# A linear recurrence with its GpSimd steps moved to ScalarE and VectorE, and four memory-query units moved

## The chip, the cores and the metric

The kernel runs on one core of one Trainium2 chip. The metric is the device time of one execution in microseconds. The inputs are fp32; the large products are formed from a high and a low part of each operand (three matmuls for one product).

## The reference

The network is two transformer-like blocks behind each other over 1024 positions of width 1024. The first has two layers: one whose mixer is windowed attention, and one whose mixer is a gated linear recurrence (LRU). Beside each mixer stands a memory attention over 256 memory rows. The second block has a stick-breaking attention and a sliding window. Only the recurrent layer matters here:

```
p = h @ w_in;  xb, gate, mq = split(p)
xc = centred_depthwise_conv(xb, conv_w, conv_b)          # 4 taps
for each direction d (forward, backward):
    r = sigmoid(xc @ wa[d] + ba[d]);  i = sigmoid(xc @ wx[d] + bx[d])   # block-diagonal, 8 blocks of 128
    log_a = -8 * r * softplus(-lam[d]);  a = exp(log_a)
    u = sqrt(-expm1(2 * log_a)) * (i * xc)
    h[t] = a[t] * h[t-1] + u[t]                           # over 1024 positions
y = (h_forward + h_backward) * gelu(gate)
mo = softmax(mq @ mk / sqrt(128)) @ mv                    # 4 heads
x = x + concat(y, mo) @ w_out;   then an MLP
```

`-expm1(2 log_a)` is computed in the kernel as `(a*a + 1) * tanh(8 r softplus)`.

## The kernel before, in words

All tiles have the 128 partitions as channels and up to 1024 positions along the free axis. The recurrent layer runs over 8 channel blocks `c` of 128. For each block there are four helpers:

- `lru_p` loads two weight pieces (512 KB each), splits each into a high and a low part (VectorE does both for these), and runs 4 x 24 = 96 matmuls of 128x512 into the tile `psx`; ScalarE copies the results to `xb` (convolution input) and `gl` (gate).
- `lru_c` is the convolution (VectorE, lines 902 and 905), and the split of its result into `xch` and `xcl`.
- `lru_g` is the gates: 24 matmuls into `psg` (8 results, each in one of the three PSUM banks with the tag `S`), and 8 sigmoids on ScalarE (line 923).
- `lru_e` is the recurrence: for both directions `exp` (line 932) and `tanh` (933) on ScalarE, the square of `a` (935) and the product `i*xc` (937) on GpSimd, `(sq+1)*r` (936) on VectorE; then `gelu` (939) and two `sqrt` (941) on ScalarE, the product `i*r` (945) and the two scans (947, 949) on VectorE, the sum of both directions (952) on GpSimd, and the product with the gate (953) and the split into `yh` and `yl` on VectorE and ScalarE, which go to DRAM.

In the sources `lru_p` of block c+1 stands before `lru_g` of block c, and `lru_c` of block c+1 before `lru_e` of block c. The sigmoids, exponentials, tanh, gelu and sqrt are tied into one order on ScalarE by `chain`, since ScalarE loads another function table at each change of function set. The rest of the order on each engine comes from the framework's scheduler, which orders instructions by their place in the sources and by simulated times.

The buffers matter. The tags `r` and `i` have three tiles each, and a block needs two of each: the second direction of block c+1 can write its gates only when the first direction's tiles of block c are free, `r` after line 952, `i` (which becomes `y`) after the split into `yl`. The tag `sq` has one tile.

The memory attention has 8 units (4 heads x 2 halves of the positions) from `mem_units`: `part_p` is the query (24 matmuls into `psq`, split into `mqh` and `mql`), `part_s` the scores (12 matmuls into `ms`, in two banks of the tag `S`; line 381 is the exponential), `part_b` transposes and the product with the values. In the sources units 0 to 3 have their queries in the last block, before its `lru_e`, and the scores of unit 0 too; the other four queries stand in the loop behind the recurrence.

After that `down_groups` multiplies with `w_out` (tile `psd`) in three groups of four 128-channel chunks: channels 0 to 511 of the recurrence, channels 512 to 1023, memory. Its first two groups load their input into the SBUF tiles that held the layer's input `hh`, `hl`, so they can be loaded only when the last query matmul has read these.

Of the kernel before, what the change touches and what calls it, by code (L numbers as in the profile page):

```python
# [47 lines left out]
def net_kernel(ctx: ExitStack, tc: tile.TileContext, xT, memT, vecs, pos, sinks, invf, mask0, maskc, alibi,  # L48
# [286 lines left out]

    def mem_units(l, hh, hl, pieces, tp, psp, order, qtag=("mqh", "mql")):
        sc = 1.0 / math.sqrt(128.0)
# [27 lines left out]
        def part_s(h, th, qh, ql):  # L365
# [5 lines left out]
            for u in range(2):  # L371
# [7 lines left out]
                for j in range(2):  # L379
                    t = 2 * u + j  # L380
                    act.activation(p[:, t, :], s2[:, j, :], AF.Exp, bias=mx[:, t:t + 1], scale=sc,
                                   accum_out=sm[:, t:t + 1])
            dve.reciprocal(sm, sm)
# [440 lines left out]
    sp8 = cp.tile([P, 16], F32, tag="sp8", name="sp8")  # L824
    nsp8 = cp.tile([P, 16], F32, tag="nsp8", name="nsp8")

    def softplus(tk):
# [17 lines left out]
        dve.tensor_scalar(out=sp8, in0=sp8, scalar1=8.0, scalar2=None, op0=ALU.mult)  # L845
        dve.tensor_scalar(out=nsp8, in0=sp8, scalar1=-1.0, scalar2=None, op0=ALU.mult)

    cond = cp.tile([P, 8], F32, tag="cond", name="cond")
# [8 lines left out]
    for l in range(2):  # L857
        if l == 1:

            with ExitStack() as ph:  # L860
# [66 lines left out]
                def lru_e(c, xc, gl, ri):  # L927
                    av = []
                    for d in range(2):
                        r, ii = ri[d]  # L930
                        a = T.tile([P, S], F32, "a", nm("a"))
                        chain(act.activation(a, r, AF.Exp, scale=nsp8[:, 8 * d + c:8 * d + c + 1]))
                        chain(act.activation(r, r, AF.Tanh, scale=sp8[:, 8 * d + c:8 * d + c + 1]))
                        sq = T.tile([P, S], F32, "sq", nm("sq"))
                        pool.tensor_tensor(out=sq, in0=a, in1=a, op=ALU.mult)
                        dve.scalar_tensor_tensor(out=r, in0=sq, scalar=1.0, in1=r, op0=ALU.add, op1=ALU.mult)
                        pool.tensor_tensor(out=ii, in0=ii, in1=xc, op=ALU.mult)
                        av.append(a)
# [12 lines left out]
                    y = ri[0][1]  # L951
                    pool.tensor_tensor(out=y, in0=ri[0][0], in1=ri[1][0], op=ALU.add)
                    dve.tensor_tensor(out=y, in0=y, in1=gl, op=ALU.mult)
# [6 lines left out]

                M = Tags({"mqh": mq, "mql": mq}, {"st": 12, "pt": 4, "mqh": 4, "mql": 4})
                mus = mem_units(1, hh, hl, w_mq[4:8], M, psp, [(i // 2, i % 2) for i in range(8)])
                pq = []
                pn = lru_p((0, 1))
                cn = lru_c(0, pn[0][0])
                for c in range(KC):
                    gl, cc = pn.pop(0)[1], cn
                    if 0 < c < KC - 1:
                        pn += lru_p((c + 1,))
                    ri = lru_g(c, cc[1], cc[2])  # L970
                    if c + 1 < KC:
                        cn = lru_c(c + 1, pn[0][0])
                    else:
                        pq = [mus[i][2]() for i in range(4)]
                        mem_units.load_w(2)
                        pre.close()
                        mk = side_pool(ph, "amk", "right")
                        M.pool.update({tag: mk for tag in ("mkh", "mkl", "mv", "mP", "st")})
                        nxt = mus[0][3](pq[0])
                    lru_e(c, cc[0], gl, ri)  # L980
                lru.close()
                xe = side_pool(down, "x1e", "left")
# [3 lines left out]
                for i in range(8):  # L986
                    cur = nxt
                    if i < 8 - 4:
                        pq.append(mus[4 + i][2]())
                    if i < 7:  # L990
# [470 lines left out]
```

## Time and profile before

| | |
|---|---|
| median of 3 runs | 3113.42 us (3112.48 to 3114.47) |
| the profiled execution's own time | 3114.57 us |
| its span, first to last instruction | 3112.6 us |
| TensorE matmuls busy | 2994.6 us, 96% |
| VectorE busy | 1803.7 us, 58% |
| ScalarE busy | 1300.7 us, 42% |
| GpSimd busy | 391.9 us, 13% |
| mean granted TensorE clock | 0.981 |

The recurrent mixer, from its first matmul to the first one of its output projection, runs from 1261 to 1590 us of the span. TensorE's busy time counts pipelined matmuls that overlap, so the share of busy time overstates how full it is: how many matmuls start in a stretch tells more.

### The profile page before, as it was taken

To read this page: it belongs to the slowest core of one execution; us is meant where nothing else is said; L and a number is where in the kernel's file an instruction comes from. 1 tells how busy PE (TensorE), PEld (TensorE's weight loads), DVE (VectorE), ACT (ScalarE), POOL (GpSimd) and SP (SyncE) were. 2 spreads that over 40 slices of the span, in tenths; PEclk is the share of its full clock that TensorE was granted. 3 is DMA by queue.
4 is the path that set the end of the run, shared out by engine and by line. 5 is a ranking of instruction groups with operands and counts; after the bars stand their busy time and mean duration, and the time that the engine had idled before them with its cause. 6 is when DMAs were issued, how large, how long until landed. Compare 5 with 4: busy or idle time off the path is not lost. (4 is left out here: it accounts for less than half of the span.)

```text
span 3112.6 us, 38989 instructions
## 1 busy us (share of the span) xinstructions
PE 2994.6 (96%) x14688; PEld 2430.1 (78%) x14688; DVE 1803.7 (58%) x3071; ACT 1300.7 (42%) x2390; POOL 391.9 (13%) x426
## 2 busy tenths in 40 slices
PE   8999999799999999999889889999999899999998
PEld 7888778678888888777667768888888677777777
DVE  8666754774456542788764674445243745555555
ACT  6566541544542221366751444451121433334442
POOL 3222100300000000243310300000001201111102
PEclk9999999999999999999999989999999899999999
DMA  7111354343365432221263333354231210111142
GB/s 265 36 55 55 101 194 150 125 149 102 108 215 194 143 115 71 68 68 65 78 254 139 119 129 109 109 181 151 68 123 54 81 55 35 35 35 48 62 176 75
DMA packets 136348, 341.61 MB, mean 110 GB/s; under 512 B 14944, under 2 KB 29664, under 8 KB 136160
## 3 DMA queue, kind: packets, MB, share of 16 engines
q1 hardware_dynamic: 131840, 331.93, 31.1%
q10 hardware_dynamic: 4320, 7.20, 0.7%
q8 instruction: 115, 1.88, 0.2%
q14 instruction: 73, 0.60, 0.1%
HBM read 245.22 MB, written 93.85 MB: 109 GB/s over the span
## 5 line engine op out<-in xcount | busy, mean ns | idle before, releaser
L122 PE MATMUL psd<-uh,wh 128*128 128x512 f32 (+1 forms) x1568 | 606.2, 387 | 2.5 <-DVE mql L105 1.7
L126 PE MATMUL psd<-uh,wl 128*128 128x512 f32 (+1 forms) x1568 | 606.5, 387 | 0.0
L125 PE MATMUL psd<-ul,wh 128*128 128x512 f32 (+1 forms) x1568 | 606.3, 387 | 0.0
L104 ACT CAST wh<-wr 128x1024 fp32r<-128x1024 f32 (+2 forms) x236 | 234.7, 998 | 730.6 <-PE psd L125 506.3
L105 DVE TENSOR_TENSOR wl<-wr,wh 128x1024 fp32r<-128x1024 f32 (+2 forms) x260 | 314.4, 1212 | 218.1 <-ACT wh L104 216.9
L316 DVE TENSOR_TENSOR x<-x,psd 128x512 f32<-128x512 f32 x288 | 196.1, 685 | 377.7 <-PE psd L126 372.6
L122 PEld LDWEIGHTS psd<-uh,wh 128*128 128x128 f32 x1568 | 294.6, 188 | 63.8 <-issue 2.3
L126 PEld LDWEIGHTS psd<-uh,wl 128*128 128x128 f32 x1568 | 294.6, 188 | 60.7 <-issue 2.6
L125 PEld LDWEIGHTS psd<-ul,wh 128*128 128x128 f32 x1568 | 294.6, 188 | 59.7 <-issue 1.7
L122 PE MATMUL psu<-oph,wh 128*128 128x512 f32 x512 | 200.4, 394 | 41.1 <-ACT wh L104 41.1
L154 POOL TENSOR_TENSOR acc<-acc,sq 128x512 f32<-128x512 f32 (+1 forms) x70 | 95.8, 1369 | 1009.5 <-ACT sq L150 998.3
L125 PE MATMUL psu<-opl,wh 128*128 128x512 f32 x512 | 199.8, 391 | 0.0
L126 PE MATMUL psu<-oph,wl 128*128 128x512 f32 x512 | 198.6, 390 | 0.0
L125 PE MATMUL pj<-hl,wh 128*128 128x512 f32 x416 | 166.1, 404 | 8.0 <-DVE hl L105 8.0
L122 PE MATMUL pj<-hh,wh 128*128 128x512 f32 x416 | 168.4, 409 | 2.5 <-DVE qkl L105 1.3
L126 PE MATMUL pj<-hh,wl 128*128 128x512 f32 x416 | 167.0, 406 | 0.0
L122 PEld LDWEIGHTS psu<-oph,wh 128*128 128x128 f32 x512 | 96.6, 189 | 62.4 <-ACT wh L104 42.0
L125 PEld LDWEIGHTS psu<-opl,wh 128*128 128x128 f32 x512 | 96.7, 189 | 20.3 <-issue 0.5
L126 PEld LDWEIGHTS psu<-oph,wl 128*128 128x128 f32 x512 | 96.6, 189 | 20.3
L1201 DVE TENSOR_TENSOR_SCAN om<-om 128x128 f32<-128x128 f32 (+7 forms) x64 | 86.0, 1352 | 38.5 <-ACT om L1197 38.3
L122 PE MATMUL psx<-hh,wh 128*128 128x512 f32 x256 | 99.0, 397 | 4.8 <-ACT gl L897 4.8
L122 PE MATMUL psu<-oph,vh 128*128 128x512 f32 x256 | 100.7, 393 | 0.0
(337 smaller groups left out, 6027.9 us busy)
## 6 DMA issues: line engine op xcount, KB each, us to landing
wr<-in_w_up SPq DMA_DIRECT2D x64, 512.0 KB, 3.8
ud<-cc SPq DMA_DIRECT2D x128, 256.0 KB, 2.2
ur<-ud SPq DMA_DIRECT2D x64, 512.0 KB, 3.4
wr<-in_w_down SPq DMA_DIRECT2D x64, 512.0 KB, 4.1
wr<-in_w_out SPq DMA_DIRECT2D x32, 512.0 KB, 3.6
wr<-in_w_in SPq DMA_DIRECT2D x26, 512.0 KB, 3.5
wra<-in_w_ada SPq DMA_DIRECT2D x24, 512.0 KB, 4.3
uh<-mixh SPq DMA_DIRECT2D x20, 512.0 KB, 7.6
```

Source lines behind the costliest of these rows:

```text
L104: act.copy(hi, src)
L105: lo_eng.tensor_tensor(out=lo, in0=src, in1=hi.bitcast(F32), op=ALU.subtract)
L122: ins = pe.matmul(out, lh, rh, start=start and i == 0, stop=False, skip_group_check=skip)
L125: pe.matmul(out, lh, rl, start=False, stop=False, skip_group_check=skip)
L126: ins = pe.matmul(out, ll, rh, start=False, stop=stop and i == n - 1, skip_group_check=skip)
L154: pool.tensor_tensor(out=self.acc[:, :n], in0=self.acc[:, :n], in1=sq[:, :n], op=ALU.add)
L316: dve.tensor_tensor(out=xs, in0=xs, in1=ps, op=ALU.add)
L1201: dve.tensor_tensor_scan(out=om[:, :nk][:, ::-1], data0=om[:, :nk][:, ::-1], data1=om[:, :nk][:, ::-1], initial=1.0, op0=ALU.mult, op1=ALU ...
```

## The change

The square of `a` becomes a second exponential of the same `r` on ScalarE (with twice the factor, kept in a new small tile `nsp16`). The products `i*xc` and the sum of both directions become VectorE instructions. GpSimd keeps only the memsets in this stage. `chain` now also holds the exponentials of this layer's memory attention, in the order of the sources. The queries of units 0 and 1 move to block 3, those of units 2 to 5 to the last block, 6 and 7 stay in the loop behind; the tags `mqh` and `mql` get 6 tiles in place of 4; the scores of unit 0 move behind the last `lru_e`, and the early load of a third query weight (`load_w(2)`) goes.

```diff
-    def mem_units(l, hh, hl, pieces, tp, psp, order, qtag=("mqh", "mql")):
+    def mem_units(l, hh, hl, pieces, tp, psp, order, qtag=("mqh", "mql"), chain=lambda ins: None):
...
-                    act.activation(p[:, t, :], s2[:, j, :], AF.Exp, bias=mx[:, t:t + 1], scale=sc,
-                                   accum_out=sm[:, t:t + 1])
+                    chain(act.activation(p[:, t, :], s2[:, j, :], AF.Exp, bias=mx[:, t:t + 1], scale=sc,
+                                         accum_out=sm[:, t:t + 1]))
...
+        dve.tensor_scalar(out=nsp16, in0=sp8, scalar1=-2.0, scalar2=None, op0=ALU.mult)
...
                     for d in range(2):
                         r, ii = ri[d]
                         a = T.tile([P, S], F32, "a", nm("a"))
+                        sq = T.tile([P, S], F32, "sq", nm("sq"))
                         chain(act.activation(a, r, AF.Exp, scale=nsp8[:, 8 * d + c:8 * d + c + 1]))
+                        chain(act.activation(sq, r, AF.Exp, scale=nsp16[:, 8 * d + c:8 * d + c + 1]))
                         chain(act.activation(r, r, AF.Tanh, scale=sp8[:, 8 * d + c:8 * d + c + 1]))
-                        sq = T.tile([P, S], F32, "sq", nm("sq"))
-                        pool.tensor_tensor(out=sq, in0=a, in1=a, op=ALU.mult)
+                        dve.tensor_tensor(out=ii, in0=ii, in1=xc, op=ALU.mult)
                         dve.scalar_tensor_tensor(out=r, in0=sq, scalar=1.0, in1=r, op0=ALU.add, op1=ALU.mult)
-                        pool.tensor_tensor(out=ii, in0=ii, in1=xc, op=ALU.mult)
...
-                    pool.tensor_tensor(out=y, in0=ri[0][0], in1=ri[1][0], op=ALU.add)
+                    dve.tensor_tensor(out=y, in0=ri[0][0], in1=ri[1][0], op=ALU.add)
...
-                M = Tags({"mqh": mq, "mql": mq}, {"st": 12, "pt": 4, "mqh": 4, "mql": 4})
-                mus = mem_units(1, hh, hl, w_mq[4:8], M, psp, [(i // 2, i % 2) for i in range(8)])
+                M = Tags({"mqh": mq, "mql": mq}, {"st": 12, "pt": 4, "mqh": 6, "mql": 6})
+                mus = mem_units(1, hh, hl, w_mq[4:8], M, psp, [(i // 2, i % 2) for i in range(8)], chain=chain)
...
                     else:
-                        pq = [mus[i][2]() for i in range(4)]
-                        mem_units.load_w(2)
                         pre.close()
                         mk = side_pool(ph, "amk", "right")
                         M.pool.update({tag: mk for tag in ("mkh", "mkl", "mv", "mP", "st")})
-                        nxt = mus[0][3](pq[0])
+                    pq += [mus[i][2]() for i in {3: (0, 1), 7: (2, 3, 4, 5)}.get(c, ())]
                     lru_e(c, cc[0], gl, ri)
+                nxt = mus[0][3](pq[0])
...
-                    if i < 8 - 4:
-                        pq.append(mus[4 + i][2]())
+                    if i < 2:
+                        pq.append(mus[6 + i][2]())
```

## Rows read from the trace of the kernel before

**Rows 1.** The page: span, busy time of each engine.
```profile
span 3112.6 us, 38989 instructions
PE 2994.6 (96%) x14688; PEld 2430.1 (78%) x14688; DVE 1803.7 (58%) x3071; ACT 1300.7 (42%) x2390; POOL 391.9 (13%) x426
```

**Rows 2.** Busy time by stretch of the span (from:to, length, then PE, PEld, DVE, ACT, POOL busy us with instruction counts, granted TensorE clock, DMA share, GB/s): one full stretch, the ramp of the recurrent mixer, three stretches of two blocks each, its end, and what comes behind.
```profile
1300.00:1340.00 40.00, 40.00 (x178) 33.14 (x177) 26.55 (x25) 19.24 (x24) 8.64 (x7) 1.00 0.21 66
...
1261.00:1354.00 93.00, 88.92 (x388) 72.24 (x387) 67.27 (x74) 40.01 (x54) 20.99 (x19) 0.98 0.16 51
1354.00:1419.00 65.00, 56.24 (x231) 44.93 (x230) 57.27 (x40) 43.24 (x52) 25.46 (x14) 0.94 0.20 69
1419.00:1484.00 65.00, 58.30 (x236) 47.01 (x235) 56.46 (x41) 42.82 (x51) 25.51 (x12) 0.92 0.21 73
1484.00:1548.00 64.00, 55.94 (x228) 44.10 (x227) 49.67 (x35) 48.74 (x59) 23.96 (x11) 0.95 0.23 79
1548.00:1590.00 42.00, 33.91 (x163) 28.14 (x163) 30.39 (x44) 29.85 (x50) 14.10 (x6) 0.88 0.42 140
1590.00:1740.00 150.00, 147.92 (x678) 118.08 (x677) 69.77 (x129) 38.33 (x83) 9.44 (x7) 1.00 0.51 189
```

**Rows 3.** Groups of TensorE instructions between 1261 and 1590 us (busy us, mean ns, idle time just before them and who ended it).
```profile
L122 PE MATMUL psx<-hh,wh 128*128 128x512 f32 x256 | 99.0, 397 | 4.8 <-ACT gl L897 4.8
L122 PE MATMUL psg<-xch,wh 128*128 128x512 f32 x64 | 27.6, 442 | 18.7 <-ACT r L923 18.7
L122 PE MATMUL psq<-hh,wh 128*128 128x512 f32 x64 | 26.6, 416 | 2.7 <-DVE mql L105 2.7
L122 PE MATMUL ms<-mkh,mqh 128*128 128x256 f32 x18 | 5.5, 321 | 8.1 <-ACT mp L381 7.7 <-ACT a L932 0.4
```

**Rows 4.** GpSimd in order of time: the sum of both directions, line 952, which comes once in each block (first, third, seventh and eighth of 8; start us, length us).
```profile
1354.10 2.39 POOL L952 TENSOR_TENSOR i<-r,r 128x1024 f32<-128x1024 f32 x1 [8.87 <-DVE r L949]
...
1419.20 2.37 POOL L952 TENSOR_TENSOR i<-r,r 128x1024 f32<-128x1024 f32 x1 [7.54 <-DVE r L949]
...
1547.54 3.23 POOL L952 TENSOR_TENSOR i<-r,r 128x1024 f32<-128x1024 f32 x1 [9.74 <-DVE r L949]
...
1584.45 2.39 POOL L952 TENSOR_TENSOR i<-r,r 128x1024 f32<-128x1024 f32 x1 [16.23 <-DVE r L949]
```

**Rows 5.** One period, 1419 to 1452 us, on GpSimd, VectorE (DVE) and ScalarE (ACT): rows of the three engines' lists, put in order of time (start us, length us).
```profile
1421.53 2.41 POOL L937 TENSOR_TENSOR i<-i,xc 128x1024 f32<-128x1024 f32 x1
1421.60 3.42 DVE L953 TENSOR_TENSOR i<-i,gl 128x1024 f32<-128x1024 f32 x1 [2.55 <-POOL i L952]
1427.05 1.28 ACT L923 ACTIVATE i<-psg,vec 128x512 f32<-128x512 f32 x2
1429.29 1.28 ACT L932 ACT_TABLE_LOAD   x1
1430.58 1.16 ACT L932 ACTIVATE a<-r,nsp 128x1024 f32<-128x1024 f32 x1
1431.88 2.75 POOL L935 TENSOR_TENSOR sq<-a 128x1024 f32<-128x1024 f32 x1 [0.68 <-ACT a L932]
1437.68 1.22 DVE L936 SCALAR_TENSOR_TENSOR r<-sq,r 128x1024 f32<-128x1024 f32 x1
1439.04 2.80 POOL L935 TENSOR_TENSOR sq<-a 128x1024 f32<-128x1024 f32 x1 [4.41 <-DVE r L936]
1444.04 1.21 DVE L936 SCALAR_TENSOR_TENSOR r<-sq,r 128x1024 f32<-128x1024 f32 x1
1445.29 1.06 ACT L941 ACTIVATE r<-r 128x1024 f32<-128x1024 f32 x1 [5.07 <-DVE r L936]
1449.43 2.28 DVE L949 TENSOR_TENSOR_SCAN r<-a,i 128x1024 f32<-128x1024 f32 x1
```

**Rows 6.** Groups of instructions between 1300 and 1600 us on VectorE and ScalarE, in the same columns as rows 3.
```profile
L945 DVE TENSOR_TENSOR i<-i,r 128x1024 f32<-128x1024 f32 x16 | 25.5, 1593 | 3.1 <-ACT r L941 3.1
L953 DVE TENSOR_TENSOR i<-i,gl 128x1024 f32<-128x1024 f32 x8 | 25.0, 3131 | 17.0 <-POOL i L952 17.0
L105 DVE TENSOR_TENSOR xcl<-xc,xch 128x1024 fp32r<-128x1024 f32 x8 | 18.2, 2273 | 2.8 <-ACT xch L104 2.8
L105 DVE TENSOR_TENSOR wl<-wr,wh 128x1024 fp32r<-128x1024 f32 x20 | 32.1, 1607 | 4.4 <-ACT wh L104 3.9
L923 ACT ACTIVATE r<-psg,vec 128x512 f32<-128x512 f32 x32 | 20.5, 685 | 31.2 <-POOL i L952 28.3 <-PE psg L126 2.9
L932 ACT ACTIVATE a<-r,nsp 128x1024 f32<-128x1024 f32 x16 | 18.3, 1146 | 0.1
```

**Rows 7.** The last block on ScalarE in order of time: three of the four table loads that lie between its exponentials of the memory attention (line 381) and its square roots (941).
```profile
1567.02 1.28 ACT L381 ACT_TABLE_LOAD   x1
...
1571.72 1.28 ACT L381 ACT_TABLE_LOAD   x1
...
1576.36 1.28 ACT L941 ACT_TABLE_LOAD   x1
```

**Rows 8.** TensorE in order of time: the last matmul of the last query, the last score matmul ahead of the output projection, and the projection's first matmul.
```profile
1586.81 0.39 PE L126 MATMUL psq<-hh,wl 128*128 128x512 f32 x1
...
1589.59 0.28 PE L126 MATMUL ms<-mkh,mql 128*128 128x256 f32 x1
1589.70 0.39 PE L122 MATMUL psd<-uh,wh 128*128 128x512 f32 x1
```

More of the change, by code (lines that the diff above doesn't have):

```diff
@@ L825, in net_kernel @@
     nsp8 = cp.tile([P, 16], F32, tag="nsp8", name="nsp8")
+    nsp16 = cp.tile([P, 16], F32, tag="nsp16", name="nsp16")
     def softplus(tk):
```

## The prediction

> **What bounds the kernel now.** I read the page first: TensorE's matmuls are busy for 96% of the span [rows 1], which looks as if nothing but TensorE counted. The table by stretch corrects that for the recurrent mixer. A stretch in which TensorE never rests starts 178 matmuls in 40 us, 0.225 us each [rows 2]. The three stretches from 1354 to 1548 us start 231 + 236 + 228 = 695 matmuls, worth 156 us, in 194 us: 38 us are lost, at a granted clock of 0.92 to 0.95. From 1548 to 1590 us 163 matmuls, at most 37 us of work, take 42 us at 0.88. Behind 1590 us TensorE is full again at 1.00. So this stage is not bound by TensorE, and a shorter recurrence can show in the time; all matmuls before 1590 us are 256x3 + 64x3 + 64x3 of 0.225 us and 54 scores of half the size [rows 3], some 265 us of 329. The gain can't be more than the 64 us that are left.
>
> What TensorE waits for there are the gate sigmoids (18.7 us) and, at the end, the exponentials of the scores (7.7 us) [rows 3]. ScalarE's sigmoids in their turn wait for GpSimd's sum of both directions, 28.3 us [rows 6], because the gates of the next block need the `r` tile which that sum is the last to read. So the stage is a ring: sum, gates, exponentials, squares, roots, scans, sum. Its period comes from the start times of the sum [rows 4]: (1547.54 - 1354.10) / 6 = 32.24 us, and 36.91 us for the last block. TensorE's own work in a block is 96 + 24 = 120 matmuls, 27.0 us.
>
> **What the change does to one turn of the ring.** I take the turn that begins at 1419.20 us [rows 4, 5].
>
> 1. The sum takes 2.37 us on GpSimd. On VectorE it is a product of the same shape, 1.21 us in its undisturbed cases (2.28 us for a scan is the upper bound). Saved: 1.2 us, and the hand-over between the engines, about 0.1.
> 2. The product with the gate takes 3.42 us (mean of all eight 3.131) [rows 5, 6], where the same form takes 1.21. It starts at 1421.60, beside GpSimd's `i*xc` of 1421.53 to 1423.94, and ends 1.1 us after that one has ended: it stood until GpSimd was done. With GpSimd idle it is 1.21 us. Saved: 2.2 us. The exponential `a` therefore starts not 11.4 but about 8.0 us after the sum's start.
> 3. From the start of `a` to the end of the second root, before: 1446.35 - 1430.58 = 15.8 us, in which GpSimd's squares (2.75 and 2.80 us) and late `(sq+1)*r` products lie in a row, since there is one `sq` tile. After: ScalarE runs six activations of 1.15 us, 1.05 to 1.17 from start to start (6.6 us), two table loads (2.6), a gelu and two roots (3.2): 12.4 us. The new exponential is bounded by the row of its twin, 1.146 us [rows 6], below and above, with no table load between `exp` and `tanh` of a block. Saved: 3.4 us, if the first `(sq+1)*r` is done when ScalarE comes to the second square; it can end 4.5 us after `a` starts, ScalarE is there at 4.4.
> 4. From the end of the last root to the end of the second scan, before: 1451.71 - 1446.35 = 5.4 us, with the first scan already under way. After: the first product begins one root earlier, and product, scan, product, scan end 5.7 to 6.6 us behind the last root, the second with a gate weight's split in between. Lost: about 0.7 us.
>
> Sum: 1.3 + 2.2 + 3.4 - 0.7 = 6.2 us, so the ring alone would turn in about 26 to 27 us. It can't run faster than TensorE's 27.0 us a block. VectorE is near as well. It was busy 57.27 + 56.46 + 49.67 = 163.4 us in six turns [rows 2], 27.2 each. Of this, standing behind GpSimd makes up 1.9 (gate product), 2 x 0.4 (`i*r`), 1.1 (`xcl`) and 2.5 x 0.4 (`wl`), by the excess of the means over 1.21 us [rows 6]: 4.8 us. The three products and sums that it gets add 3 x 1.21 = 3.6 us. It stands at 27.2 - 4.8 + 3.6 = 26.0 us a block. ScalarE gets 2.3 us more on about 22. Three engines at 26 to 27 us do not mesh without waits; I take 29 us a turn, with 27.0 as the lower and 31.0 (below, VectorE) as the upper bound.
>
> The Trainium skill (SBUF — State Buffer, Who interferes with whom) says that GpSimd and a VectorE instruction with two SBUF inputs exclude each other for a whole instruction, whoever starts first. By that rule alone all of GpSimd's instruction time might be charged to VectorE, about 12 us a block; the rows show less than half of it, as GpSimd mostly runs while VectorE has nothing due or started first. The rows decide.
>
> **The parts around the ring.** In block 0 the same steps are shorter, but it starts with VectorE and TensorE still at the layer's first blocks: 2 us (0 to 4). In the last block the exponentials of the scores no longer lie between tanh and the roots. Four table loads of 1.28 us between 1567 and 1578 us [rows 7] become one, 3.85 us, and there is no next block to prepare: I take 27 us for it, against 36.91, a gain of 9.9 (6 to 12).
>
> The Trainium skill (ScalarE: Activation LUTs, What ACT_TABLE_LOAD costs) puts 2.66 us on a switch, since it counts a drain behind the load. Here `a` starts 1.29 us behind the start of its load [rows 5], so no such drain is seen; by the page the last block would gain 4 us more.
>
> The moved queries. Units 0 and 1 put 48 matmuls, 10.8 us, ahead of block 5's `psx` on TensorE, and a 512 KB weight on SP's queue with one cast and one subtraction on ScalarE and VectorE. They are hidden by what TensorE loses today, 6.3 us a turn, but not wholly once a turn is 29 us: that is a reason why I don't take 27. The last block keeps units 2 to 5, 96 matmuls and 24 of the gates, 27 us: as long as that block. Units 6 and 7 wait for query tiles of units 0 and 1, so for their scores; those of unit 1 need a bank that the exponentials of unit 0 free, now behind the last root. The last query then ends some 8 us behind the last root, as does the ring itself. In the old order it ended at 1587.2 us, 3 us after the last sum began (1584.45), and the projection began at 1589.7 [rows 4, 8]. So the start of the projection follows the last sum in both. Fewer scores are done by then, about 24 matmuls against 54. The other 30, at 0.12 us (half of 0.225 us, as they have half the columns), have to be fitted into a full TensorE: with the banks that they change, 4 us lost (0 to 9). The pinned exponentials are otherwise covered: the projection's first two groups need no memory output, and are 2 x 16 x 12 matmuls, 86 us. `nsp16` is one tiny instruction in the first layer's MLP, covered by TensorE there.
>
> **Sum.** 2 + 6 x (32.24 - 29.0) + 9.9 - 4 = 27.3 us. The profiled execution took 3114.57 us (its span is 3112.6, 2.0 us lie around it; the median of the runs is 1.2 us less): 3087 us.
>
> **Rivals.**
>
> *More: TensorE alone is the bound.* Turns of 27.0 us and waits at the end gone: 2 + 31.4 + 12 - 2 = 43 us, 3071. For it speaks the clock, which rises from 0.93 as the waits go; against it that three engines would have to mesh. Chance 0.10.
>
> *Less: VectorE's order is the bound.* If VectorE keeps its idle 5.0 us a turn (32.2 - 27.2) beside 26.0 us of work, a turn is 31.0 us: 2 + 7.4 + 5.9 - 4 = 11 us, 3103. A like time comes out if the ring gains as forecast, but the last two queries (10.8 us) lie wholly behind it: 27.3 - 10.8 = 16.5 us, 3098. Chance 0.19.
>
> *Nothing, or slower: ScalarE stands before the second square.* The one `sq` tile makes that exponential wait for the first `(sq+1)*r`, and in a pinned order nothing else of the chain gets past; sigmoids, hence TensorE's banks, and the copies of `psx` wait behind it. Today that product ends 8.3 us after `a` starts (1438.90 - 1430.58) [rows 5], behind convolution and weight splits. If VectorE's order stays like that with the two `i*xc` products ahead too, it ends at 10.7, and ScalarE waits 6.3 us: a turn is 33 us, and with the last block's gain the whole comes to 3116, no change. If the second such product is held as today as well (behind an `i*r` and a tap of the convolution, 2.5 us), a turn is 35.8 us: 3132. It decides from about 6 us of wait a turn. Against it: the first `(sq+1)*r` has nothing to wait for but ScalarE, and the 4.8 us a block that VectorE stood behind GpSimd no longer push it back. Chance 0.08 for no change, 0.08 for slower.
>
> **Chances and range.** Forecast, a gain of 18 to 38 us: 0.55. With the two faster cases, faster by over 0.2% (6.2 us, about what a measurement tells from no change) has 0.84, same 0.08, slower 0.08. The range runs from the case with TensorE alone, 3071, to the edge between the smaller gain and no change, 3109; it leaves out the no-change and slower cases and small ends of the others. The forecast's own range is 3077 to 3097.
>
> **What the changed profile would show.** The sum of both directions every 28 to 30 us on VectorE, and the last one at about 1553 us; the gate product at 1.2 us, `xcl` and `wl` near 1.2; no wait of ScalarE for a GpSimd instruction; the wait of a root for `(sq+1)*r` gone, and none over 2 us in its place before the second square; TensorE's clock from 1354 to 1548 us above 0.95; one table load between gelu and the roots of the last block; the projection's first matmul near 1560 us. I am wrong if the period is above 31 us, above all if ScalarE's idle time moves to line 936's product, or if the projection starts more than 10 us after the last sum.

## The result: slower, 3155.4 us against 3113.7

The changed kernel takes 3155.41 us (median of 4 runs, 3154.57 to 3157.59), the kernel before 3113.72 us in the same series: ratio 1.0135, with a 95% interval of 1.0118 to 1.0153. I had said 3087 us. Yet the ring does turn as fast as forecast where nothing else was put into it. Two things went wrong. The first has nothing to do with the recurrence: every large matmul of the whole kernel got 2.7% slower, since a tile of 64 bytes moved the weights in SBUF against the matmuls' other operand. The second would have undone most of the gain by itself: the queries put into block 3 stand in the way of the ring and cost their whole length, and what is won before the output projection is partly lost at its beginning.

The page of the changed kernel: its span, and the busy time of each engine (as [rows 1]).

```profile
span 3152.8 us, 38979 instructions
PE 3042.2 (96%) x14688; PEld 2426.5 (77%) x14688; DVE 1783.8 (57%) x3096; ACT 1315.9 (42%) x2403; POOL 293.8 (9%) x386
```

TensorE starts as many matmuls as before, and is busy 47.6 us longer with them; the span has grown by 40.2 us. The time of the removed GpSimd work (98 us) is gone from POOL's row.

The sum of both directions, now on VectorE (line 954), in the changed kernel: blocks 0, 2, 3, 4, 6 and 7 in order of time, as [rows 4].

```profile
1371.81 1.23 DVE L954 TENSOR_TENSOR i<-r,r 128x1024 f32<-128x1024 f32 x1
...
1430.01 1.23 DVE L954 TENSOR_TENSOR i<-r,r 128x1024 f32<-128x1024 f32 x1
1459.49 1.22 DVE L954 TENSOR_TENSOR i<-r,r 128x1024 f32<-128x1024 f32 x1
1499.81 1.22 DVE L954 TENSOR_TENSOR i<-r,r 128x1024 f32<-128x1024 f32 x1
...
1561.85 1.21 DVE L954 TENSOR_TENSOR i<-r,r 128x1024 f32<-128x1024 f32 x1
1593.59 1.22 DVE L954 TENSOR_TENSOR i<-r,r 128x1024 f32<-128x1024 f32 x1
```

Blocks 1 to 3 turn in (1459.49 - 1371.81) / 3 = 29.2 us, where I had taken 29. The next turn, from the sum of block 3 to that of block 4, takes 40.3 us; I call it the long turn. The two behind it take 31.0 us on average, the last block 31.7.

Busy time by stretch in the changed kernel, in the columns of [rows 2]: two turns, one turn, the long turn, two turns, the last block, and the first 46 us behind the last sum.

```profile
1371.00:1430.00 59.00, 57.02 (x238) 45.22 (x237) 51.30 (x46) 47.91 (x56) 0.64 (x4) 0.97 0.23 81
1430.00:1459.00 29.00, 29.00 (x126) 23.25 (x125) 21.13 (x21) 20.78 (x25) 0.00 (x0) 1.00 0.22 73
1459.00:1500.00 41.00, 39.41 (x170) 31.42 (x169) 31.51 (x31) 27.89 (x33) 0.14 (x2) 1.00 0.22 73
1500.00:1562.00 62.00, 55.83 (x229) 44.15 (x228) 46.13 (x42) 52.97 (x63) 0.00 (x0) 0.94 0.26 88
1562.00:1594.00 32.00, 22.37 (x93) 18.19 (x92) 22.13 (x26) 24.28 (x36) 0.00 (x0) 0.79 0.88 317
1594.00:1640.00 46.00, 38.95 (x199) 29.48 (x198) 31.86 (x84) 20.79 (x66) 0.00 (x0) 0.96 0.56 203
```

In the turn from 1430 us TensorE has no rest (29.00 of 29.00 us, granted clock 1.00). The same stretches for the instructions of the queries (`psq`) alone: matmuls, weight loads, VectorE, ScalarE, then clock and DMA as above.

```profile
1430.00:1459.00 29.00, 6.31 (x26) 4.49 (x24) 1.37 (x2) 1.15 (x2) 1.00 0.22 73
1459.00:1500.00 41.00, 0.00 (x0) 0.00 (x0) 0.00 (x0) 0.00 (x0) 1.00 0.22 73
```

And for those of the gates (`psg`) alone: matmuls, weight loads, ScalarE.

```profile
1430.00:1459.00 29.00, 1.72 (x6) 1.12 (x6) 2.55 (x4) 1.00 0.22 73
1459.00:1500.00 41.00, 10.71 (x42) 7.81 (x42) 7.68 (x12) 1.00 0.22 73
```

So of the queries moved to block 3 one half runs in the turn from 1430 us, the other half just before it, and none in the long turn. What they push into the long turn is the gates: 42 gate matmuls start there, where a block has 24. In the last block TensorE starts 93 matmuls in 32 us at a clock of 0.79, and behind the last sum it still isn't full (38.95 of 46 us, 0.96), where the kernel before was nearly so at 1.00 [rows 2].

Groups of TensorE, VectorE and ScalarE instructions of the changed kernel between 1279 and 1594 us, as [rows 3, 6].

```profile
L122 PE MATMUL psg<-xch,wh 128*128 128x512 f32 x64 | 25.5, 409 | 5.5 <-ACT r L925 5.5
L122 PE MATMUL psq<-hh,wh 128*128 128x512 f32 x64 | 26.7, 417 | 4.2 <-DVE mql L105 4.2
L122 PE MATMUL ms<-mkh,mqh 128*128 128x256 f32 x12 | 4.4, 392 | 7.9 <-ACT mp L381 4.4 <-DMA mkh<-mkhd 3.5
L105 DVE TENSOR_TENSOR xcl<-xc,xch 128x1024 fp32r<-128x1024 f32 x8 | 9.7, 1218 | 0.0
L955 DVE TENSOR_TENSOR i<-i,gl 128x1024 f32<-128x1024 f32 x7 | 8.5, 1221 | 0.1
L936 ACT ACTIVATE sq<-r,nsp 128x1024 f32<-128x1024 f32 x16 | 18.3, 1145 | 3.6 <-DVE r L939 3.6
```

The gate matmuls' wait for the sigmoids has fallen from 18.7 to 5.5 us. The gate product takes 1.221 us (before 3.131), `xcl` 1.218 (2.273). The wait that I feared most, ScalarE before the second square, comes to 3.6 us over all 16 squares.

The beginning of the output projection in the changed kernel: its first matmul on TensorE, the loads of the residual tiles `x` on SP's queue, and VectorE's first addition to them (start us, length us; in brackets the idle time before and who ended it).

```profile
1579.22 0.80 PE L122 MATMUL psd<-uh,wh 128*128 128x512 f32 x1 [1.11 <-DVE mql L105]
...
1602.68 5.58 SPq L530 DMA_DIRECT2D x<-xd  x8
...
1609.19 0.69 DVE L316 TENSOR_TENSOR x<-x,psd 128x512 f32<-128x512 f32 x1 [5.58 <-DMA x<-xd]
```

The projection begins 14.4 us before the last sum, but its results can leave PSUM only by an addition to `x`, and that comes 30.0 us behind its first matmul. In the kernel before it was 17.5 us (1589.70 to 1607.21).

### The profile page after: what moved, and what is told of

It is laid out like the page before. It is cut to its first block, busy times and chain, and to the rows that moved or that the text cites. A ratio compares the mean times of both kernels' runs of the same rounds, so it can differ in the third digit from the quotient of the medians.

```text
span 3152.8 us, 38979 instructions
## 1 busy us (share of the span) xinstructions
PE 3042.2 (96%) x14688; PEld 2426.5 (77%) x14688; DVE 1783.8 (57%) x3096; ACT 1315.9 (42%) x2403; POOL 293.8 (9%) x386
## 5 line engine op out<-in xcount | busy, mean ns | idle before, releaser
L122 PE MATMUL psd<-uh,wh 128*128 128x512 f32 (+1 forms) x1568 | 618.2, 394 | 7.2 <-DVE x L316 5.5
L125 PE MATMUL psd<-ul,wh 128*128 128x512 f32 (+1 forms) x1568 | 616.6, 393 | 0.0
L126 PE MATMUL psd<-uh,wl 128*128 128x512 f32 (+1 forms) x1568 | 616.1, 393 | 0.0
L105 DVE TENSOR_TENSOR wl<-wr,wh 128x1024 fp32r<-128x1024 f32 (+2 forms) x260 | 306.9, 1183 | 235.0 <-ACT wh L104 233.9
L122 PE MATMUL psu<-oph,wh 128*128 128x512 f32 x512 | 203.4, 400 | 40.2 <-ACT wh L104 40.2
L125 PE MATMUL psu<-opl,vh 128*128 128x512 f32 x256 | 102.2, 399 | 0.0
```

What stands on the lines that cost most here:

```text
L105: lo_eng.tensor_tensor(out=lo, in0=src, in1=hi.bitcast(F32), op=ALU.subtract)
L122: ins = pe.matmul(out, lh, rh, start=start and i == 0, stop=False, skip_group_check=skip)
L125: pe.matmul(out, lh, rl, start=False, stop=False, skip_group_check=skip)
L126: ins = pe.matmul(out, ll, rh, start=False, stop=stop and i == n - 1, skip_group_check=skip)
```

## Experiments

Times below are medians; each series had runs of the kernel before beside it, at 3113.7 to 3114.3 us, and gains are taken against these. "Matmul pace" is the mean distance from start to start of dense 512-column matmuls, worked out from the trace (some 9,300 pairs in each kernel). SBUF addresses are those at which the program places a tile in a partition.

### The 64 bytes alone, and the change without them

`a_pad64` is the kernel before with the new tile and its one instruction, which nothing reads:

```diff
+    nsp16 = cp.tile([P, 16], F32, tag="nsp16", name="nsp16")
...
+        dve.tensor_scalar(out=nsp16, in0=sp8, scalar1=-2.0, scalar2=None, op0=ALU.mult)
```

> The kernel before, plus the 64 bytes per partition of the tile nsp16 and the one small instruction that writes it; nothing reads it. The recurrence and the queries are as before. Theory (the tile moves the weight tiles by 64 bytes in SBUF, and with these addresses every 512-column matmul starts 6.7 ns later): dense matmuls start every 233.3 ns in place of 226.7, and the time is 3113 + 45 (what the changed kernel lost outside the recurrent layer) + 8 = 3160 to 3170 us. Rival (the slower pace of the matmuls comes from the order of instructions or another trait of the changed program): pace 226.7 ns and 3113 us.

Measured: 3161.31 us (3159.3 to 3164.12), ratio 1.0149 (1.0134 to 1.0164): 47.1 us slower, with nothing of the change in it but a tile. Matmul pace 233.3 ns against 227.2. Where it shows is a stretch of the first layer's MLP, 700 to 800 us, which the change doesn't touch; columns as in [rows 2]. The kernel before:

```profile
700.00:800.00 100.00, 100.00 (x443) 82.81 (x442) 43.19 (x56) 46.38 (x71) 0.00 (x0) 1.00 0.30 100
```

The changed kernel:

```profile
700.00:800.00 100.00, 100.00 (x431) 80.55 (x430) 43.92 (x57) 44.93 (x69) 0.00 (x0) 1.00 0.29 101
```

The kernel before with the 64 bytes:

```profile
700.00:800.00 100.00, 100.00 (x430) 80.61 (x429) 44.92 (x59) 46.86 (x73) 0.00 (x0) 1.00 0.30 102
```

All three have TensorE busy for all of the 100 us at a granted clock of 1.00, and two of them get 12 or 13 matmuls fewer through. Neither busy time nor clock tells that; the count does.

`b_noshift` is the whole change, with `nsp16` kept in 16 columns of a tile that is there already:

```diff
-    nsp16 = cp.tile([P, 16], F32, tag="nsp16", name="nsp16")
+    nsp16 = kk.rearrange("p a b -> p (a b)")[:, 0:16]
```

> The changed kernel, with nsp16 put into 16 columns of the tile kk, which is no longer needed by then, so that no tile moves. Theory (addresses): dense matmuls start every 226.7 ns, and the rest of the change is left: 3155 - 53 = about 3102 us (3096 to 3108). Rival (other trait of the program): 233.3 ns and 3155 us.

Measured: 3109.49 us (3107.01 to 3111.82), ratio 0.9984 (0.9975 to 0.9993), pace 227.2 ns. That is 1.5 us above the range I had given for it. The change without its shift is 4.8 us faster than the kernel before, not 12 (the 3102 us of that expectation) and not 27. The shift is worth 3155.4 - 3109.5 = 45.9 us here, 47.1 us alone.

### Which addresses

The weights (`wh`) stand at 24,544 in the kernel before and at 24,608 with the 64 bytes; the moving operands (`hh`, `uh` and their like) are allotted from the other side and stay where they were, `hh` at 163,808. Three more placements, `p128`, `p64_h192` and `c_pad256`:

```diff
 # p128: kernel before
+    nsp16 = cp.tile([P, 32], F32, tag="nsp16", name="nsp16")
...
 # p64_h192: kernel before, the 64 bytes, and 192 that push the moving tiles down
+    hpad = hp.tile([P, 48], F32, tag="hpad", name="hpad")
...
+    nsp16 = cp.tile([P, 16], F32, tag="nsp16", name="nsp16")
...
 # c_pad256: the changed kernel
-    nsp16 = cp.tile([P, 16], F32, tag="nsp16", name="nsp16")
+    nsp16 = cp.tile([P, 64], F32, tag="nsp16", name="nsp16")
```

> The kernel before, with 128 bytes per partition of an extra tile in place of the 64 (same place in the allocation). Weight tiles then stand 128 bytes behind those of the kernel before, the moving tiles at their old addresses. If any shift of the weights against the old place slows the pace, dense 512-column matmuls start every 233 ns and the kernel takes about 3160 us, as with 64 bytes. If the pace depends on the relation of the two addresses in a pattern that repeats, or on one bad offset alone, it is 226.7 ns and 3114 us. No theory of mine has a firm claim here; I expect a slow pace (233 ns, 3160 us) with 6 chances in 10.

> The kernel before with 64 bytes in front of the weight tiles (as in the slow kernel) and 192 bytes of padding on the other side, so that weight tiles and moving tiles again have the same address modulo 256. If the relation of the two addresses decides, dense matmuls start every 226.7 ns again and the kernel takes about 3114 us. If the weights' own address decides, the pace stays at 233.3 ns and the time near 3160 us. I expect the first.

> The changed kernel as it is, with 256 bytes per partition for its new small tile in place of 64, so that everything behind it stands 256 bytes further than before the change, not 64. If only the addresses modulo 256 count, dense matmuls start every 227 ns as in the kernel before and it takes what the changed kernel without the shift took, 3109 us (3107 to 3112). If any shift slows it: 233 ns and 3155 us.

| kernel | `wh` at | `hh` at | both modulo 256 | pace, ns | us |
|---|---|---|---|---|---|
| before | 24,544 | 163,808 | 224, 224 | 227.2 | 3113.9 |
| `a_pad64` | 24,608 | 163,808 | 32, 224 | 233.3 | 3161.3 |
| after | 24,608 | 163,808 | 32, 224 | 233.3 | 3155.4 |
| `p128` | 24,672 | 163,808 | 96, 224 | 232.4 | 3156.4 |
| `p64_h192` | 24,608 | 163,616 | 32, 32 | 227.2 | 3110.2 |
| `b_noshift` | 24,544 | 163,808 | 224, 224 | 227.2 | 3109.5 |
| `c_pad256` | 24,800 | 163,808 | 224, 224 | 227.2 | 3105.3 |

`p64_h192` tells it: with the weights at the address of the two slow kernels, and the moving tiles moved by as much modulo 256, the pace is back. The same stretch in this kernel:

```profile
700.00:800.00 100.00, 100.00 (x443) 82.81 (x442) 43.34 (x55) 46.61 (x72) 0.00 (x0) 1.00 0.30 100
```

So it isn't the weights' own address; what counts is where they stand in relation to the moving operand. The changed kernel itself has a cross-check: the dense matmuls of the memory projection at its beginning (26 to 66 us) have both operands behind the new tile, so that both moved by 64 bytes, and they still start every 228.1 ns. Equal modulo 256 was fast in all four kernels of the table that have it, a difference of 64 or 128 slow in all three. My expectation for `p128` (slow, 6 in 10) held. What in the chip does it, and whether 256 is the true period, stays open: other distances were not tried. `p128`, `p64_h192` and `c_pad256` are one run each; the 46 us between the two groups are far more than the 2 to 8 us over which runs of one kernel scatter here. `c_pad256` is 4 us below `b_noshift`; I make nothing of that difference.

### The recurrence alone, and the queries alone

`d_rec_only` has the new recurrence without the shift, with queries, scores and `chain` of the kernel before; `e_queries_only` has the other half, with GpSimd's squares, products and sums. Their edits are the diff's `lru_e` part and its `mem_units` and loop part.

> The kernel before with the new recurrence alone (squares on ScalarE, products and sum on VectorE; nsp16 in kk, so no tile moves); queries, their buffers and the order of the memory exponentials as before. Theory: the turns of the ring take 29 to 30 us as in the changed kernel's undisturbed blocks, no turn of 40 us since no query stands in block 3, and the output projection starts some 30 us earlier: 3080 to 3092 us. Rival (the moved queries are needed for any gain, since TensorE runs out of work in the last block): 3105 to 3114 us.

Measured: 3107.91 us (3105.45 to 3111.01), ratio 0.9979 (0.997 to 0.9989): 6.3 us faster, a miss of some 20 us. The sums of blocks 0, 3, 6 and 7 in this kernel:

```profile
1350.91 1.22 DVE L954 TENSOR_TENSOR i<-r,r 128x1024 f32<-128x1024 f32 x1
...
1438.46 1.22 DVE L954 TENSOR_TENSOR i<-r,r 128x1024 f32<-128x1024 f32 x1
...
1530.74 1.22 DVE L954 TENSOR_TENSOR i<-r,r 128x1024 f32<-128x1024 f32 x1
1566.13 1.22 DVE L954 TENSOR_TENSOR i<-r,r 128x1024 f32<-128x1024 f32 x1
```

Six turns of 29.97 us on average, against 32.24 [rows 4]: 13.6 us are won. The last block, with its four queries and the score exponentials in the middle, takes 35.4 us, hardly less than the 36.9 before. And then half of the gain is handed back: from the last sum to the 385th matmul of the projection it is 128.3 us, 120.2 in the kernel before.

> The kernel before with the moved queries alone (six query tiles, units 0 and 1 in block 3, 2 to 5 in the last block, scores of unit 0 behind it, exponentials pinned); the recurrence with GpSimd as before, no new tile. Theory: the 48 matmuls in block 3 lengthen one turn by up to 10.8 us less the TensorE idle time of a turn (6 us), and the last turn loses its extra table loads (4 us): 3110 to 3125 us. Rival (the placement gains by itself, as TensorE has more work at hand in the last block): 3095 to 3108 us.

Measured: 3127.7 us (3125.24 to 3128.57), ratio 1.004 (1.0026 to 1.0054), 13.5 us slower; just beyond what I expected. The sums of blocks 3 and 4 in this kernel, on GpSimd as in the kernel before:

```profile
1447.37 2.70 POOL L952 TENSOR_TENSOR i<-r,r 128x1024 f32<-128x1024 f32 x1 [10.18 <-DVE r L949]
1492.99 2.39 POOL L952 TENSOR_TENSOR i<-r,r 128x1024 f32<-128x1024 f32 x1 [11.21 <-DVE r L949]
```

The long turn takes 45.6 us here, against 32.5 in the kernel before, and the last block, with four queries as before but its scores behind it, 31.2 against 36.9. So the queries in block 3 cost 12 to 13 us in that turn with either recurrence (in `e_queries_only` 11.3 over it and the two turns before, one of which is shorter). I had expected TensorE's idle time to take up 6 us of them. The old recurrence still leaves that time idle, and it hid nothing. The later scores give half of the cost back.

Where the queries stand on TensorE tells why. The first gate matmul of block 4 in the changed kernel, then in `d_rec_only`:

```profile
1459.63 0.39 PE L122 MATMUL psg<-xch,wh 128*128 128x512 f32 x1
```

```profile
1425.75 0.39 PE L122 MATMUL psg<-xch,wh 128*128 128x512 f32 x1
```

With the queries ahead it starts 0.1 us behind the sum of block 3 (1459.49), without them 12.7 us ahead of it (1438.46). The exponential `a` of block 4 then starts 19.6 us behind that sum, against 9.1. In `e_queries_only` it is 23.8 us, in the kernel before 11.9. This is read from the traces; no run changes that order alone.

### Only the two queries moved, and the tail

`h_early_x` is `d_rec_only` with two of the eight `x` tiles loaded ahead of the last block, into SBUF that is free there, and used first (SP issues the two loads as early as 1284 us):

```diff
...
+                xe0 = side_pool(down, "x1e0", "left")
+                x01 = [xe0.tile([P, S], F32, tag=f"x{c}", name=nm("x")) for c in range(2)]
...
+                        load_x(x01, x_d[0])
+                        early[0] = True
...
+                x = x01 + [xe.tile([P, S], F32, tag=f"x{c}", name=nm("x")) for c in range(2, KC)]
+                load_x(x[2:], x_d[0], 2)
...
+                    if early[0]:
+                        todo = [(0, 0), (0, 1)] + [t for t in todo if t[0]]
```

> The new recurrence alone, without the shift, with the queries and scores of the kernel before; added: two of the eight residual tiles x are loaded ahead of the last block into SBUF that is free there, and the first of the three projection groups takes both halves of these two first. If the projection stands because its results cannot leave PSUM until x has come (about 15 us between its first matmul and the first addition of x), 48 more matmuls fit into that wait: 10.9 us at most, less what the memory units use of it; I expect 3100 us (3096 to 3104). If it stands for its own inputs or for TensorE work of the memory units, nothing changes: 3107 to 3109 us.

Measured: 3096.03 us (3094.5 to 3096.92), ratio 0.9943 (0.9927 to 0.996). It is 17.9 us faster than the kernel before and the fastest of all. The recurrence in it is as long as in `d_rec_only` (the last sum starts 306.8 us behind the stage's first matmul, 306.7 there); the 11.9 us between the two kernels are won behind it, 8.1 of them up to the 385th matmul of the projection; where the other 3.8 come from I haven't traced. VectorE's first additions to `x` behind the recurrence, in `d_rec_only`:

```profile
1594.17 0.69 DVE L316 TENSOR_TENSOR x<-x,psd 128x512 f32<-128x512 f32 x1 [7.24 <-DMA x<-xd]
```

and in `h_early_x`:

```profile
1575.47 0.69 DVE L320 TENSOR_TENSOR x<-x,psd 128x512 f32<-128x512 f32 x1
1594.29 0.69 DVE L320 TENSOR_TENSOR x<-x,psd 128x512 f32<-128x512 f32 x1 [1.84 <-DMA x<-xd]
```

Both projections begin at 1570.2 to 1570.4 us. In `d_rec_only` TensorE then stands until that first addition has freed a bank:

```profile
1594.91 0.79 PE L122 MATMUL psd<-uh,wh 128*128 128x512 f32 x1 [5.39 <-DVE x L316]
```

In `h_early_x` it waits for no addition to `x` there; the longest wait is 1.0 us, for `mql`. What it gives TensorE, by stretch, first in `d_rec_only`:

```profile
1566.00:1595.00 29.00, 22.06 (x113) 16.39 (x111) 15.68 (x39) 11.59 (x34) 0.00 (x0) 0.97 1.01 377
1595.00:1640.00 45.00, 45.00 (x200) 35.07 (x201) 22.70 (x53) 12.24 (x34) 0.00 (x0) 0.94 0.40 152
```

then in `h_early_x`:

```profile
1570.00:1582.00 12.00, 10.98 (x53) 8.63 (x52) 6.62 (x14) 2.76 (x5) 0.00 (x0) 1.00 1.02 363
1582.00:1595.00 13.00, 12.65 (x79) 9.61 (x77) 8.84 (x26) 8.34 (x29) 0.00 (x0) 1.00 1.02 412
1595.00:1640.00 45.00, 45.00 (x197) 34.12 (x196) 23.23 (x47) 11.75 (x28) 0.00 (x0) 1.00 0.50 184
```

The first has a granted clock of 0.97 in the stretch with the pause and 0.94 behind it, where ten matmuls in a row start 0.43 us apart in place of 0.23; the second has 1.00 throughout. From the last sum to the 385th projection matmul it is now 120.3 us, as in the kernel before. So the loss of 8.1 us behind the recurrence was the wait for `x` (5.4 us) and the lower clock behind it: with two tiles early, and used first, both are gone. The two early tiles are also 1 MB less to move while the DMA engines are full, some 2.6 us at about 400 GB/s (an estimate); what this, the early landing and the order are worth each wasn't separated.

`k_xq` has the other six loads of `x` issued by GpSimd, past SP's queue:

```diff
-                load_x(x[2:], x_d[0], 2)
+                for c in range(2, KC):
+                    nc.gpsimd.dma_start(x[c], x_d[0][:, c, :])
```

> The kernel with the new recurrence and two early x tiles (3096.0 us), with the loads of the other six x tiles issued by GpSimd, which is idle there, so that they need not stand behind the second group's inputs on SP's queue (issued 1584.7 to 1590.8 us there). If their place in that queue is what the first additions wait for, they are issued near 1581 us and it takes 3091 to 3094 us. If the DMA engines themselves are full there (382 to 429 GB/s behind 1580 us), the order only shifts who waits: 3095 to 3098.

Measured: 3098.17 us (3095.22 to 3100.66), ratio 0.9948 (0.9931 to 0.9964): no gain over `h_early_x`. GpSimd's loads of `x` in this kernel:

```profile
1507.91 0.75 POOL L995 DMA_DIRECT2D x<-xd  x1 [79.00 <-DVE i L944]
1541.74 0.54 POOL L995 DMA_DIRECT2D x<-xd  x1 [33.07 <-DMA mkl<-mkld]
1567.83 2.20 POOL L995 DMA_DIRECT2D x<-xd  x4 [25.55 <-ACT mp L385]
```

They leave 19 to 77 us earlier than in `h_early_x` (1584.70 us for the first), more than I expected, and it is worth nothing. By itself that says little about the DMA: in `h_early_x` TensorE no longer waited for `x`, so earlier loads had no wait to shorten. The run does show that SBUF for these six tiles is free by 1569.5 us; what holds their loads until 1584.70 us in `h_early_x` is their place on SP's queue. The DMA engines are busy all the time from 1570 to 1595 us, in this kernel too:

```profile
1570.00:1582.00 12.00, 10.98 (x54) 8.61 (x53) 6.49 (x14) 2.42 (x5) 0.03 (x1) 1.00 1.02 382
1582.00:1595.00 13.00, 12.65 (x79) 9.75 (x78) 11.01 (x32) 8.55 (x30) 0.00 (x0) 1.00 1.03 380
```

`j_q01` is `h_early_x` with the queries of units 0 and 1 in block 3, those of units 2 and 3 in the last block:

```diff
-                        pq = [mus[i][2]() for i in range(4)]
+                        pq += [mus[i][2]() for i in (2, 3)]
...
+                    if c == 3:
+                        pq = [mus[i][2]() for i in (0, 1)]
```

> The kernel with the new recurrence and two early x tiles (3096.0 us; block-3 turn 29.6 us, last turn 35.5), in which only the queries of units 0 and 1 (48 matmuls, 10.8 us) move from the last block to block 3. If they were hidden by time that TensorE loses there, as my prediction had it, the block-3 turn stays below 33 us and the last turn shortens to 25 to 30 us: 3086 to 3090. If TensorE has no room in block 3 at a turn of 29.6 us, that turn grows by 11 to 12 us and the last one shrinks by 5 to 10: 3097 to 3103. If the last turn does not shrink at all: 3108.

Measured: 3104.83 us (3101.72 to 3109.17), ratio 0.997 (0.9957 to 0.9983): 8.8 us slower than without the move. The sums of blocks 3, 4, 6 and 7:

```profile
1438.55 1.22 DVE L960 TENSOR_TENSOR i<-r,r 128x1024 f32<-128x1024 f32 x1
1478.72 1.22 DVE L960 TENSOR_TENSOR i<-r,r 128x1024 f32<-128x1024 f32 x1
...
1540.94 1.22 DVE L960 TENSOR_TENSOR i<-r,r 128x1024 f32<-128x1024 f32 x1
1571.88 1.20 DVE L960 TENSOR_TENSOR i<-r,r 128x1024 f32<-128x1024 f32 x1
```

The block-3 turn takes 40.2 us (29.7 without the move), the last one 30.9 (35.5). 10.5 us are paid, about the 10.8 that 48 matmuls are worth, and 4.5 saved: the last block is held by more than the number of its queries. The time came out 2 us above the range that I had given for this case.

### The scores

`i_scores_free` is `b_noshift` with the scores of unit 0 ahead of the last `lru_e` again, and the memory exponentials out of `chain`:

```diff
-[(i // 2, i % 2) for i in range(8)], chain=chain)
+[(i // 2, i % 2) for i in range(8)])
...
+                    if c == KC - 1:
+                        nxt = mus[0][3](pq[0])
                     lru_e(c, cc[0], gl, ri)
-                nxt = mus[0][3](pq[0])
```

> The changed kernel without the shift of addresses, with its queries at their new places (blocks 3 and last), but with the scores of unit 0 ahead of the last block's recurrence again and the memory exponentials untied from the order on ScalarE. If the late, tied scores are what gives the gain back behind the last block (they fall into the time in which the projection should run), the first 384 projection matmuls are done some 8 us earlier than without this edit, and it takes about 3101 us (3097 to 3105). If the exponentials then cost table loads inside the last recurrence, as in the kernel before, it is unchanged, 3108 to 3111 us.

Measured: 3113.33 us (3110.51 to 3114.72), ratio 0.9998 (0.9989 to 1.0007), 3.8 us slower than `b_noshift` and above both of my ranges. My theory of the tied scores falls: the last turn grows from 30.9 to 35.7 us, and the 385th projection matmul comes no earlier (440.2 us behind the stage's first one, 439.4 in `b_noshift`). To place and pin the scores behind the last roots is a gain of its own in that block.

## Why the prediction was wrong, step by step

The working in one table: gains in us against the kernel before. The rows are read from the sums' start times; the tail runs from the last sum to the 385th projection matmul.

| step | forecast | `b_noshift` | `d_rec_only` | `h_early_x` |
|---|---|---|---|---|
| block 0 | 2 | 1.6 | 1.7 | 1.6 |
| six turns | 19.4 | 1.3 | 13.6 | 13.6 |
| last block | 9.9 | 6.0 | 1.5 | 1.5 |
| behind it | -4 | -4.5 | -8.1 | 0.0 |
| sum | 27.3 | 4.4 | 8.7 | 16.6 |
| measured in the time | | 4.8 | 6.3 | 17.9 |

**The step that failed outright** is the one that I costed at nothing: "`nsp16` is one tiny instruction in the first layer's MLP, covered by TensorE there". The instruction is covered. Its tile isn't an instruction: it moved the weights by 64 bytes against their moving operands, which costs 6.1 ns on each dense matmul, some 60 us over the 9,978 of 512 columns, of which 46 to 47 us reach the end. This alone turns the sign: without it the change is 4.8 us faster. I had priced what the engines do with the tile and not what its allocation does to everything allotted behind it.

**The queries in block 3** were mis-sized. I let them be "hidden by what TensorE loses today, 6.3 us a turn, but not wholly". None of them was hidden: the long turn grew by 12.1 us in `b_noshift` (41.7 us against 29.7 in `d_rec_only`), by 10.5 us in `j_q01`, and by 13.1 us (11.3 with the two turns before) in `e_queries_only`, where the old recurrence still leaves TensorE its idle time; 48 matmuls are worth 10.8. My sum counted that idle time twice, since at a turn of 29 us TensorE has only 2 us of it left. But `e_queries_only` shows that this isn't the cause. I had written myself that the queries stand ahead of block 5's `psx` on TensorE; I hadn't seen that they stand ahead of the gates of block 4 too, a step of the ring. As the traces read, the idle time lies where TensorE waits for the ring, and matmuls that stand ahead of the ring's own step delay it by their whole length.

**The turn** was right: 28.2, 29.8, 29.6 and 29.7 us for the first four in `d_rec_only`, 28.2, 30.1 and 29.5 for the first three of the changed kernel. The size of its parts was a little low each: in the turn of 1430.01 us `a` starts 9.1 us behind the sum (8.0 forecast), the second root ends 13.4 us later (12.4), the second scan 5.8 us behind it (5.7 to 6.6), and the next sum starts 1.2 us after that, since VectorE does a step of the next convolution first (line 904, 0.81 us): 29.5 in all. The allowance from 27 to 29 us covered this. The last two of the six turns missed it in `d_rec_only`, 30.4 and 32.2 us: there the queries of the last block have already begun (from 1488.6 us), TensorE waits once for their split (`mql`, 3.4 us; another 9.2 in the last block), and the sigmoids of `i` wait for the gates' matmuls behind them (3.5 us).

**The price beside GpSimd** was right: gate product 1.22 us, `xcl` and `wl` 1.22, no ScalarE wait for GpSimd in the recurrence. So was the wait before the second square, 0.25 us in the turn quoted, and 0.23 us on average. The rival that put 6 us there can be struck out: the kernel got slower, but not by that road.

**The last block** was to take 27 us and takes 31.7. Its one table load between gelu and the roots came true, and `i_scores_free` shows that this part is worth 4.8 us. The rest of the miss is in the same three pieces: 9.9 us from the sum to `a`, 14.2 to the end of the last root, 7.7 to the next sum.

**Behind the recurrence** my -4 us came out as -4.5, for another reason; that the sizes agree is luck. I priced 30 scores more in a full TensorE. In truth TensorE isn't full there. "The start of the projection follows the last sum" held in `d_rec_only` (4.3 us behind it) but not in the changed kernel (14.4 us ahead), and it isn't what counts: the projection fills its banks and stands until `x` has come. In the kernel before TensorE doesn't wait for `x` behind the last sum; the first addition comes 22.8 us behind it. In `d_rec_only` it comes 28.0 us behind: SP issues the loads of `x` only from 1583.42 us on, behind those of the projection's inputs, with the DMA engines full (share 1.01). `h_early_x` takes the wait away there. In the changed kernel TensorE's longest wait behind the last sum is for `x` too, 4.7 us, but no run removed it in that kernel.

The Trainium skill (ScalarE: Activation LUTs, What ACT_TABLE_LOAD costs) counts a drain with each load. In the changed kernel, as before, `a` starts 1.29 us behind the start of its load (1439.07 - 1437.78); no run here shows the drain.

## What to carry to other kernels

A new tile is priced twice: by its instructions, and by what its bytes do to the addresses of all that is allotted behind it; after any change of allocation, compare how many matmuls start in a full stretch that the change doesn't touch before reading anything else. Idle time of an engine hides moved work only if that work doesn't stand ahead of the next step of the ring that sets the time: here 48 matmuls, worth 10.8 us, lengthened one turn by 10.5 to 13.1 us with either recurrence. When a stage is shortened, follow its end to the next thing that is waited for, here the loads of `x`, which stood behind other loads while the DMA engines were full, and move that too: it was worth more (11.9 us) than the shorter stage alone (6.3 us).

## What the hardware showed that I had not expected

TensorE's pace in fp32r matmuls depends on where the stationary and the moving operand stand to each other in SBUF: 227.2 ns from start to start with both at the same address modulo 256, 232.4 to 233.3 ns with 64 or 128 bytes between, at a granted clock of 1.00 and 100% busy in either case. Busy time hides it, since the records overlap: a 100 us stretch reads 100.00 with 443 matmuls and with 430.

The second is that a wait of TensorE costs more than its own length. In `d_rec_only` it stands 5.39 us, and then starts matmuls 0.43 us apart until 1600 us, at a granted clock of 0.5 (1.2 GHz), in place of 0.23 at 1.00 (2.4 GHz). The wait and some 3 us for these matmuls (an estimate: half of the 5.8 us for which this lasts) make up the 8.1 us by which the stretch to the 385th matmul grew.
